# Jensen-Shannon divergence on one core: two first fp32 loads in place of three, products apart from row group 2 on, and new ranges and orders

## Chip, cores and metric

The kernel runs on one core of a Trainium2 chip. The metric is device time in microseconds (us). A profile's span covers the instructions alone and is about 2 us shorter than the time of its run. A run that is more than 1.5% above the fastest of its kernel counts as slow. Medians are over all runs, ratios and their intervals over fast runs alone, and all profiles are of fast runs. Names: ACT is ScalarE, DVE is VectorE, PE is TensorE (PEld its loading of weights), POOL is GpSimd, SP is SyncE.

## The reference

`p` and `q` are 1024 x 4096, fp32.

```python
m = 0.5 * (p + q)
kl_pm = np.sum(p * np.log(p / (m + 1e-8) + 1e-8), axis=-1)
kl_qm = np.sum(q * np.log(q / (m + 1e-8) + 1e-8), axis=-1)
return (0.5 * (kl_pm + kl_qm)).astype(np.float32)
```

The kernel takes log p, log q and log(p+q) apart, so each element pair costs three logs on ACT.

## The kernel before

Eight row groups g of 128 rows; a group's columns are cut into loads, log ranges (for log p and log q together) and sum ranges (for p+q). The order on each engine is written down by hand, one letter per operation:

- `q` (ACT): logs of a range of p and q. `c` (ACT): log of a sum.
- `F` (PE): the sum p+q, by identity matmuls, into one of two PSUM buffers. `a` (DVE): the same for the first fp32 loads.
- `x` (DVE): subtract the logs, then multiply. In "apart" groups `m` (DVE) multiplies inputs and logs, and `s` (DVE) multiplies the sum by its log and reduces.
- `r` (PE): adds a product's columns up in PSUM. `f` (DVE): reduces that to a row's result.

```python
psp = ctx.enter_context(tc.tile_pool(name="psp", bufs=2, space=bass.MemoryType.PSUM))  # sums
AB_BUFS = 3
...
def op_F(j):
    g, c0, w = parts[j]
    st = psp.tile([P, SW], fp32, tag="s")
    v = pq(g, c0, w)
    for b in range(0, w, MMN):
        m = min(MMN, w - b)
        for t in range(2):
            nc.tensor.matmul(out=st[:, b : b + m], lhsT=ident, rhs=v[:, t, b : b + m],
                             start=t == 0, stop=t == 1)
...
def op_m(i):
    g, c0, w = logs[i]
    u = pq(g, c0, w)
    if i < NL - FUSED_LAST:
        nc.vector.tensor_tensor(out=u, in0=u, in1=ab[i], op=Alu.mult)  # over the inputs
        product["m", i] = u
        return
...
def psum_before(j):            # what F(j) needs: its PSUM buffer's last reader
    if j - 2 < HW:
        return []
    return [("s" if apart(parts[j - 2]) else "c", j - 2)]
```

A product `m` is written over the inputs, so it must wait until every `F` that reads those columns is done. And in an apart group a sum `F(j)` must wait until DVE's `s(j-2)` has read the PSUM buffer; in the other groups ACT's `c(j-2)` is enough.

Of the kernel before, what the change touches and what calls it, by code (L numbers as in the profile page):

```python
# [15 lines left out]


LOADS = [
    [256, 320, 384, 512, 704, 832, 1088],
    [1280, 1408, 1408],  # L20
    [1536, 1280, 1280],
    [2048, 2048],
# [3 lines left out]
    [2048, 2048],  # L26
]
LOGS = [
    [256, 320, 384, 512, 704, 832, 1088],
    [1280, 1408, 1408],  # L30
    [1536, 2560],
    [1536, 2560],
    [2048, 2048],
    [768, 1408, 1920],
    [2432, 1664],
    [1664, 1024, 1280, 128],
]
SUMS = [
    [256, 320, 384, 512, 704, 832, 1088],
    [1280, 1408, 1408],  # L40
    [1536, 1408, 1152],
    [1536, 1280, 1280],
    [1152, 1536, 1408],
    [1536, 1152, 1408],
    [1408, 1536, 1152],
    [1280, 1536, 1280],
]
HW = 3

APART = 4  # L50
FUSED_LAST = 1


# [2 lines left out]


ACT_ORDER = """
q0 c0 q1 c1 q2 c2 q3 c3 q4 c4 q5 c5 q6 c6 q7 c7 q8 c8 q9 c9 q10 c10 q11 c11 c12 q12 c13
q13 c14 c15 q14 c16 c17 q15 c18 c19 q16 q17 c20 c21 q18 c22 q19 c23 c24 q20 q21 c25 c26  # L60
q22 q23 c27 q24
"""
PE_ORDER = """
r0 F3 r1 F4 r2 r3 F5 r4 F6 r5 F7 r6 F8 F9 r7 F10 r8 r9 F11 F12 r10 F13 r11 F14 F15 r12 r13
F16 F17 r14 r15 F18 F19 r16 r17 F20 F21 F22 r18 F23 r19 r20 F24 r21 F25 F26 r22 r23 F27
r24 r25
"""
DVE_ORDER = """
a0 a1 x0 a2 x1 x2 x3 x4 x5 x6 x7 f0 x8 x9 x10 f1 x11 x12 x13 f2 x14 x15 s16 s17 m14 m15
s18 s19 m16 m17 s20 s21 f3 f4 m18 s22 f5 m19 s23 s24 m20 m21 s25 s26 m22 f6 m23 s27 f7 m24  # L70
"""


# [1 line left out]
def kernel(  # L75
# [6 lines left out]
    nc = tc.nc  # L82
# [15 lines left out]
    qv = q.rearrange("(p g) d -> g p d", g=n_rg)  # L98
    ov = out.rearrange("(p g) -> p g", g=n_rg)

    def ranges(widths):

        r = []
        for g in range(n_rg):
            col = 0
            for w in widths[g]:
                r.append((g, col, w))
                col += w
            assert col == n_cols
        return r  # L110

    loads, logs, parts = ranges(LOADS), ranges(LOGS), ranges(SUMS)
    assert loads[:HW] == logs[:HW] == parts[:HW]
    split = loads[HW][1]
    NL, NS = len(logs), len(parts)
# [12 lines left out]
    early = []  # L128
    for i in range(HW):
        t32 = small.tile([P, 2, loads[i][2]], fp32, tag=f"pq32_{i}")  # L130
# [6 lines left out]
    def pq(g, c0, w):  # L137
        if g == 0:
            for i in range(HW):
                if loads[i] == (g, c0, w):  # L140
                    return early[i]
            c0 -= split
            assert c0 >= 0
        return data[g][:, :, c0 : c0 + w]
# [4 lines left out]
    nc.vector.memset(epsc_t, SHIFT * 1e-8)  # L149
    for i in range(HW):  # L150
        g, c0, w = loads[i]
        nc.sync.dma_start(out=early[i][:, 0, :], in_=pv[g, :, c0 : c0 + w])
        eng = nc.scalar if i < 2 else nc.sync
        eng.dma_start(out=early[i][:, 1, :], in_=qv[g, :, c0 : c0 + w])
    warm = small.tile([P, 1], fp32, tag="warm")
    nc.scalar.activation(out=warm, in_=tiny_t, func=Act.Ln, bias=tiny_t, scale=1.0)  # L156
    ident = small.tile([P, P], fp16, tag="ident")
    make_identity(nc, ident)
    for g, c0, w in loads[HW:]:
        v = pq(g, c0, w)  # L160
# [4 lines left out]
        out=half, in0=ident, scalar1=0.5, scalar2=0.0, op0=Alu.mult, op1=Alu.add  # L165
# [6 lines left out]

    apart = lambda r: r[0] >= APART
    terms = [("x", j) for j in range(NS) if not apart(parts[j])]
# [105 lines left out]
    def op_f(g):  # L280
        if g < APART:
            nc.vector.tensor_reduce(  # L282
                out=res[:, g : g + 1], in_=acc[g][:, :AW], axis=AX, op=Alu.add
            )
            return
        before, now = next_run(g)
        if g < n_rg - 1:
            now = res[:, g : g + 1]
        junk = small.tile([P, AW], fp16, tag="junk")
        nc.vector.tensor_tensor_reduce(  # L290
            out=junk, in0=acc[g][:, :AW], in1=ones, scale=1.0, scalar=before,
            op0=Alu.mult, op1=Alu.add, accum_out=now,
        )
# [32 lines left out]
    while any(queues):  # L326
        moved = False
        for todo in queues:
            while todo and all(d in emitted for d in after[todo[0][0]](todo[0][1])):
                kind, i = todo.pop(0)  # L330
# [42 lines left out]
```

## Time and profile before

| | before |
|---|---|
| time, median | 106.2 us |
| ACT busy | 93.0 of 103.0 us |
| DVE busy | 82.1 us |
| PE busy | 66.9 us |
| idle of ACT before logs of sums | about 0 |
| loads land until | 85.2 us |

The profiled run took 105.1 us, 1.1 us under the median. From the page of the kernel before: the span, the busy times, the busy tenths of ACT and the granted clock of PE (in tenths of full speed) in 40 slices, and the shares of the chain that ended last.

```profile
span 103.0 us, 1163 instructions
...
PE 66.9 (65%) x412; PEld 41.1 (40%) x412; DVE 82.1 (80%) x87; ACT 93.0 (90%) x55; POOL 22.0 (21%) x46
...
ACT  3736999999999899999999999999999999999900
...
PEclk9999999999999859999966999999669999999995
...
DMA 56%; ACT 23%; issue 12%; POOL 4%; DVE 3%; ACTq 0%; POOLq 0%; DVEq 0%
```

ACT is busy from its start to its end but for the third and fourth slices; its work is the limit. From its timeline (start, duration, instruction, and in brackets the idle time before it and who ended it), the start, the one later wait for a load, and the last log:

```profile
8.63 0.94 ACT L215 ACTIVATE ab_t<-t,tiny_t 128x768 f16<-128x768 f32 x1 [2.47 <-DMA t<-in_q_dram]
...
35.19 4.56 ACT L215 ACTIVATE ab_t<-t,tiny_t 128x5120 f16<-128x5120 f16 x1 [0.28 <-DMA t<-in_q_dram]
...
97.44 0.59 ACT L215 ACTIVATE ab_t<-t,tiny_t 128x256 f16<-128x256 f16 x1
```

In the apart groups DVE runs two products together, and the sums for ACT's next two logs are ready before ACT asks. From the timeline of all engines:

```profile
61.23 4.49 DVE L245 TENSOR_TENSOR t<-t,ab_t 128x4096 f16<-128x4096 f16 x2
61.80 1.02 PE L203 MATMUL st<-t,ident 128*128 128x512 f16 x4
62.84 2.88 ACT L223 ACTIVATE c_t<-st,epsc_t 128x1408 f16<-128x1408 f32 x2
63.57 1.91 PE L272 MATMUL acc_t<-t,half 128*128 128x256 f16 x16 [0.75 <-DVE t L245]
```

The clock of PE falls to a half three times before the end of the work. Busy time in windows around two of them. A line gives the window, its length, the busy us (and number of instructions) of PE, PEld, DVE, ACT and POOL, then the granted clock (1.00 full, 0.50 half), the DMA share and GB/s:

```profile
31.95:35.36 3.41, 1.20 (x12) 1.08 (x12) 2.49 (x3) 3.13 (x3) 1.06 (x2) 1.00 1.10 216
35.36:38.77 3.41, 3.41 (x12) 1.35 (x10) 3.32 (x3) 3.41 (x1) 1.06 (x2) 0.50 1.06 211
...
69.50:72.90 3.40, 1.01 (x6) 0.48 (x5) 3.25 (x5) 3.40 (x4) 0.00 (x0) 1.00 1.06 212
72.90:76.32 3.42, 3.42 (x13) 1.67 (x12) 3.17 (x6) 3.42 (x2) 0.00 (x0) 0.50 1.07 214
```

A window in which PE worked 1.0 to 1.2 us is followed by one at half clock. ACT's busy time there is full: the slow matmuls delay nobody.

### The profile page before, as it was taken

The numbers are of one execution on the slowest core, as the hardware profiler recorded it, in microseconds if no ns is written. First come the engines' busy times: TensorE is split into PE (matmuls) and PEld (weight loads), VectorE is DVE, ScalarE is ACT, GpSimd is POOL, SyncE is SP. The second block draws the span as 40 slices with busy tenths as digits, with TensorE's granted clock in tenths as the row PEclk, the third lists the DMA queues.
The fourth block names the chain that finished last, engine by engine and source line by source line (L and its number), as shares of the span: only waits on it lengthen the run. The fifth ranks groups of instructions, "written<-read, shape, count | busy, mean of one in ns | idle before, by whom it ended". The sixth has DMA issues, their size and how long they took to land.

```text
span 103.0 us, 1163 instructions
## 1 busy us (share of the span) xinstructions
PE 66.9 (65%) x412; PEld 41.1 (40%) x412; DVE 82.1 (80%) x87; ACT 93.0 (90%) x55; POOL 22.0 (21%) x46
## 2 busy tenths in 40 slices
PE   0033986738772798579199877883799649865440
PEld 0010544433432535157154634741268436552330
DVE  2246976669879691999879999999997699799980
ACT  3736999999999899999999999999999999999900
POOL 7935443323232422222222221200000000000000
PEclk9999999999999859999966999999669999999995
DMA  2999999999999999999999999999999920000000
GB/s 76 271 201 183 211 212 214 210 211 210 212 209 217 211 218 212 212 216 210 218 215 212 216 213 212 215 208 221 208 213 218 202 40 6 0 0 0 0 0 2
DMA packets 6773, 17.34 MB, mean 168 GB/s; under 512 B 880, under 2 KB 2416, under 8 KB 6768
## 3 DMA queue, kind: packets, MB, share of 16 engines
q0 software_dynamic: 5760, 16.29, 81.1%
q1 hardware_dynamic: 720, 0.69, 2.3%
q10 hardware_dynamic: 288, 0.30, 0.8%
q8 instruction: 3, 0.05, 0.2%
q14 instruction: 2, 0.02, 0.0%
HBM read 33.55 MB, written 0.00 MB: 326 GB/s over the span
## 4 chain that ended last, share of the span: by engine, by line
DMA 56%; ACT 23%; issue 12%; POOL 4%; DVE 3%; ACTq 0%; POOLq 0%; DVEq 0%
DMA t<-in_p_dram 56%; ACT ab_t L215 14%; ACT c_t L223 8%; POOL t L161 2%; DVE c_t L258 1%; POOL t L162 1%; DVE t L251 0%; DVE junk L290 0%; POOL ident masks.py:199 0%; POOL ident masks.py:197 0%; ACTq L215 0%; DVE t L245 0%; POOLq masks.py:199 0%; DVEq L251 0%; DVEq L290 0%
## 5 line engine op out<-in xcount | busy, mean ns | idle before, releaser
L215 ACT ACTIVATE ab_t<-t,tiny_t 128x2816 f16<-128x2816 f16 (+17 forms) x25 | 62.0, 2500 | 3.3 <-DMA t<-in_q_dram 3.3
L272 PE MATMUL acc_t<-t,half 128*128 128x256 f16 (+1 forms) x260 | 31.8, 273 | 18.2 <-DVE t L238 10.8
L203 PE MATMUL st<-t,ident 128*128 128x512 f16 (+5 forms) x142 | 36.5, 401 | 6.5 <-DVE run L258 3.4
L272 PEld LDWEIGHTS <-half 128*128 128x128 f16 x270 | 26.4, 100 | 35.0 <-issue 29.4
L223 ACT ACTIVATE c_t<-st,epsc_t 128x1408 f16<-128x1408 f32 (+7 forms) x25 | 32.5, 1338 | 0.1
L234 DVE TENSOR_TENSOR ab_t<-ab_t,c_t 128x2560 f16<-128x2560 f16 (+10 forms) x16 | 19.6, 1222 | 7.7 <-ACT c_t L223 7.7
L203 PEld LDWEIGHTS <-ident 128*128 128x128 f16 x142 | 14.9, 109 | 22.9 <-issue 13.8
L238 DVE TENSOR_TENSOR t<-t,ab_t 128x2560 f16<-128x2560 f16 (+7 forms) x13 | 18.1, 1395 | 1.5 <-PE acc_t L272 0.5
L245 DVE TENSOR_TENSOR t<-t,ab_t 128x4096 f16<-128x4096 f16 (+7 forms) x10 | 18.3, 1849 | 0.9 <-ACT ab_t L215 0.9
L161 POOL DMA_DIRECT2D t<-in_p_dram x20 | 10.8, 541 | 23.5 <-DMA t<-in_p_dram 23.4
L162 POOL DMA_DIRECT2D t<-in_q_dram x20 | 10.7, 536 | 20.3 <-DMA t<-in_q_dram 20.3
L258 DVE CUSTOM_DVE_ANT_0 c_t<-st,c_t,run 128x1536 f16<-128x1536 f32 (+3 forms) x8 | 13.2, 1648 | 0.6
L272 PE MATMUL acc_t<-ab_t,half 128*128 128x256 f16 (+2 forms) x10 | 2.1, 356 | 7.6 <-DVE ab_t L238 7.6
L258 DVE CUSTOM_DVE_ANT_0 c_t<-st,c_t 128x1152 f16<-128x1152 f32 (+3 forms) x4 | 6.2, 1554 | 0.0
L191 DVE TENSOR_TENSOR s<-t 128x256 f32<-128x256 f32 (+2 forms) x3 | 1.5, 492 | 4.9 <-DMA t<-in_q_dram 4.9
L290 DVE CUSTOM_DVE_ANT_0 junk<-acc_t,ones,run 128x256 f16<-128x256 f32 x4 | 1.9, 480 | 1.5 <-PE acc_t L272 1.4
L156 ACT ACT_TABLE_LOAD x1 | 1.3, 1283 | 1.7 <-PEq L357 1.7
L238 DVE TENSOR_TENSOR ab_t<-t,ab_t 128x512 f16<-128x512 f32 (+2 forms) x3 | 2.5, 825 | 0.1
L282 DVE TENSOR_REDUCE res<-acc_t 128x1 f32<-128x256 f32 x4 | 1.7, 419 | 0.0
L223 ACT ACTIVATE c_t<-s,epsc_t 128x256 f16<-128x256 f32 (+2 forms) x3 | 1.6, 547 | 0.0
L258 DVE DVE_READ_ACCUMULATOR2_ANT run<- 128x1 f32 x12 | 1.0, 83 | 0.0
L147 DVE MEMSET tiny_t<- 128x1 f32 x1 | 0.1, 59 | 0.8 <-PEq L357 0.8
(14 smaller groups left out, 2.6 us busy)
## 6 DMA issues: line engine op xcount, KB each, us to landing
t<-in_p_dram POOLq DMA_DIRECT2D x10, 512.0 KB, 19.1
t<-in_q_dram POOLq DMA_DIRECT2D x10, 512.0 KB, 19.4
t<-in_p_dram POOLq DMA_DIRECT2D x3, 320.0 KB, 13.2
t<-in_q_dram POOLq DMA_DIRECT2D x3, 320.0 KB, 13.2
t<-in_p_dram POOLq DMA_DIRECT2D x2, 352.0 KB, 10.9
t<-in_q_dram POOLq DMA_DIRECT2D x2, 352.0 KB, 11.6
t<-in_p_dram POOLq DMA_DIRECT2D x1, 384.0 KB, 12.8
t<-in_q_dram POOLq DMA_DIRECT2D x1, 384.0 KB, 13.4
```

The costliest lines, as they stand in the source:

```text
L161: nc.gpsimd.dma_start(out=v[:, 0, :], in_=pv[g, :, c0 : c0 + w])
L162: nc.gpsimd.dma_start(out=v[:, 1, :], in_=qv[g, :, c0 : c0 + w])
L203: nc.tensor.matmul(out=st[:, b : b + m], lhsT=ident, rhs=v[:, t, b : b + m], start=t == 0, stop=t == 1,)
L215: nc.scalar.activation(out=ab_t, in_=pq(g, c0, w), func=Act.Ln, bias=tiny_t, scale=SHIFT)
L223: nc.scalar.activation(out=c_t[:, :w], in_=s[j], func=Act.Ln, bias=epsc_t, scale=SHIFT * 0.5)
L234: nc.vector.tensor_tensor(out=v, in0=v, in1=c[j].unsqueeze(1).to_broadcast([P, 2, w]), op=Alu.subtract)
L238: nc.vector.tensor_tensor(out=into, in0=u, in1=v, op=Alu.mult)
L245: nc.vector.tensor_tensor(out=u, in0=u, in1=ab[i], op=Alu.mult)
L258: nc.vector.tensor_tensor_reduce(out=c[j], in0=s[j], in1=c[j], scale=-0.5, scalar=before, op0=Alu.mult, op1=Alu.add, accum_out=now,)
L272: nc.tensor.matmul(out=acc[g][:, :m], lhsT=half, rhs=v[:, t, b : b + m], start=k == terms_of[g][0] and n == 0, stop=k == terms_of[g][-1] a ...
L282: nc.vector.tensor_reduce(out=res[:, g : g + 1], in_=acc[g][:, :AW], axis=AX, op=Alu.add)
L290: nc.vector.tensor_tensor_reduce(out=junk, in0=acc[g][:, :AW], in1=ones, scale=1.0, scalar=before, op0=Alu.mult, op1=Alu.add, accum_out=now,)
```

## The change

Its intent, read from the diff: start ACT's long run sooner (the first fp32 columns in two loads, p on one hardware queue and q on the other), let DVE wait less for logs of sums in groups 2 and 3, put more log work ahead of the wait for a load near 35 us, and shorten the tail by a last sum of 640 columns. Cut to its core:

```diff
 LOADS = [
-    [256, 320, 384, 512, 704, 832, 1088],
+    [320, 640, 512, 704, 896, 1024],
 ...
 SUMS = [  # LOGS likewise
 ...
-    [1280, 1536, 1280],
+    [1280, 640, 1408, 128, 640],
 ]
-HW = 3
-APART = 4
+HW = 2
+APART = 2
 PE_ORDER = """
-... r10 F13 r11 F14 F15 r12 r13
-F16 F17 r14 r15 F18 F19 r16 r17 F20 F21 F22 r18 F23 r19 r20 ...
+... r10 F13 r11 F14 r12 F15
+F16 r13 F17 F18 r14 F19 F20 r15 F21 F22 r16 F23 F24 r17 ...
 DVE_ORDER = """
-... s16 s17 m14 m15
-s18 s19 m16 m17 s20 s21 f3 f4 m18 ...
+... m10 s11 m11 s12 f2 m12 s13 s14 f3 m13 s15
+s16 m14 s17 s18 f4 m15 ...
@@ first loads
-        eng = nc.scalar if i < 2 else nc.sync
-        eng.dma_start(out=early[i][:, 1, :], in_=qv[g, :, c0 : c0 + w])
+        nc.scalar.dma_start(out=early[i][:, 1, :], in_=qv[g, :, c0 : c0 + w])
```

More of the change, by code (lines that the diff above doesn't have):

```diff
@@ L28 @@
 LOGS = [
-    [256, 320, 384, 512, 704, 832, 1088],
+    [320, 640, 512, 704, 896, 1024],
     [1280, 1408, 1408],
     [1536, 2560],
-    [1536, 2560],
     [2048, 2048],
-    [768, 1408, 1920],
-    [2432, 1664],
-    [1664, 1024, 1280, 128],
+    [2048, 2048],
+    [1920, 2176],
+    [2304, 1792],
+    [1408, 1152, 768, 640, 128],
 ]
 SUMS = [
-    [256, 320, 384, 512, 704, 832, 1088],
+    [320, 640, 512, 704, 896, 1024],
     [1280, 1408, 1408],
+    [1152, 1408, 1536],
+    [1280, 1536, 1280],
+    [1280, 1536, 1280],
     [1536, 1408, 1152],
-    [1536, 1280, 1280],
-    [1152, 1536, 1408],
-    [1536, 1152, 1408],
-    [1408, 1536, 1152],
-    [1280, 1536, 1280],
-]
-HW = 3
-APART = 4
+    [1280, 1280, 1536],
+    [1280, 640, 1408, 128, 640],
+]
+HW = 2
+APART = 2
 FUSED_LAST = 1
 ACT_ORDER = """
-q0 c0 q1 c1 q2 c2 q3 c3 q4 c4 q5 c5 q6 c6 q7 c7 q8 c8 q9 c9 q10 c10 q11 c11 c12 q12 c13
-q13 c14 c15 q14 c16 c17 q15 c18 c19 q16 q17 c20 c21 q18 c22 q19 c23 c24 q20 q21 c25 c26
-q22 q23 c27 q24
+q0 c0 q1 c1 q2 c2 q3 c3 q4 c4 q5 c5 q6 c6 q7 c7 q8 c8 q9 c9 c10 q10 c11 q11 c12 q12 c13
+c14 q13 c15 c16 q14 c17 c18 q15 c19 c20 q16 c21 c22 q17 c23 q18 c24 c25 q19 q20 c26 c27
+q21 q22 c28 q23
 """
 PE_ORDER = """
-r0 F3 r1 F4 r2 r3 F5 r4 F6 r5 F7 r6 F8 F9 r7 F10 r8 r9 F11 F12 r10 F13 r11 F14 F15 r12 r13
-F16 F17 r14 r15 F18 F19 r16 r17 F20 F21 F22 r18 F23 r19 r20 F24 r21 F25 F26 r22 r23 F27
-r24 r25
+F2 r0 F3 r1 F4 r2 r3 F5 r4 F6 r5 F7 F8 r6 F9 r7 F10 r8 r9 F11 F12 r10 F13 r11 F14 r12 F15
+F16 r13 F17 F18 r14 F19 F20 r15 F21 F22 r16 F23 F24 r17 F25 r18 F26 F27 r19 r20 F28 r21
+r22
 """
 DVE_ORDER = """
-a0 a1 x0 a2 x1 x2 x3 x4 x5 x6 x7 f0 x8 x9 x10 f1 x11 x12 x13 f2 x14 x15 s16 s17 m14 m15
-s18 s19 m16 m17 s20 s21 f3 f4 m18 s22 f5 m19 s23 s24 m20 m21 s25 s26 m22 f6 m23 s27 f7 m24
+a0 a1 x0 x1 x2 x3 x4 x5 x6 f0 x7 x8 m9 s9 s10 f1 m10 s11 m11 s12 f2 m12 s13 s14 f3 m13 s15
+s16 m14 s17 s18 f4 m15 s19 s20 m16 s21 s22 f5 m17 s23 m18 s24 s25 m19 f6 m20 s26 s27 m21
+m22 s28 f7 m23
 """
```

## The prediction

> **What bounds it now.** ScalarE. The page gives ACT 93.0 of a 103.0 us span, DVE 82.1, PE 66.9. In the timeline ACT idles only at the start (2.47 us at 6.2-8.6 for the third q load, 0.25 and 0.26 before it) and once for a load (0.28 at 35.2); otherwise it runs until 98.0. A tail of DVE sum, final sum and fused product ends at 100.7, then the store. PE and DVE have slack.
>
> **What the change does.**
> - Loads: same 960 fp32 columns, balanced over two queues. From the landings (3.5, 4.85, 8.54 us) I estimate q1's pair at about 7.2. ACT then reaches column 960 about 0.6 us earlier, but the load that row group 2 waits for (35.08) is DMA-paced; two sum logs now stand before that wait (2560 columns rather than 1536), worth about 0.85 us. Net gain at 35 us: about 0.9 us.
> - ACT: 53 logs and the same columns in both.
> - DVE: groups 2 and 3 swap a subtraction (1.36 us per 2304 elements) for a sum with reduction (1.42 per 1152 columns): about +0.1 us a tile, under 1 us in all.
> - Tail: last sum tile 640 instead of 1280 columns (1.54 us to about 0.85): about 1 us gained.
> - Order, the step that decides. From group 3 on PE has r11 F14 r12 F15 F16 r13 F17 F18: a product's accumulation stands before the sum that the next product waits for (a product overwrites what the sum reads). The sum in turn waits for a PSUM buffer that the DVE reduction frees. So a loop forms: product (2.2 us for 4096 elements) -> its 16 accumulating matmuls (1.9) -> sum F (1.25 to 1.45) -> next product, about 5.5 us with semaphores, while ACT has 4.95 for the same 2048 columns. Before, F stood ahead (F18 F19 r16 r17) and this was hidden.
>
> I laid the three queues out with durations fitted to the old trace; that reproduces the old ACT starts within 0.2 us. For the new order it gives ACT waits for PE sums before c14 (about 1.2 us), c15 (0.7), c16 to c18 (0.4 each): about 3.2 us. Balance: -0.9 -1.0 +3.2 and small terms = +1.7 us at full PE clock.
>
> **Clock.** The old trace shows half clock for 3.41 us at 35.4, 52.4 and 72.9, each just after PE had idled 2.2 to 2.4 us. The Trainium skill, "TensorE: Matmul & The Clock Gate", Part 1, says an idle window of about 3.4 us halves the clock; this trace agrees on the window's length, but a window with 1.0 to 1.3 us of work already did it. The new loop makes PE idle 2.6 us per turn and puts PE on ACT's path, so such windows now cost 1 to 1.5 us each. Three or four of them: +3 to +5 us.
>
> **Prediction: 110.8 us**, range 107.5 to 114.0. Chances: faster 0.07, same 0.15, slower 0.78.
>
> **Right if:** ACT busy stays near 93 us but with 4 to 8 us of idle before sum logs (L223), released by PE sums, between 50 and 95 us; DVE products wait for PE; more half-clock windows after 40 us; the chain of waits alternates PE and DVE there; the tail after the last log is about 1 us shorter; q1's pair lands near 7.2.
>
> **Wrong if:** ACT shows no waits on PE after 40 us (then about 104.3, 1.8% faster), the clock stays full (then about 108).

## The result and the profile after

Ratios in this document are the mean time of one kernel's fast runs over that of the other's fast runs of the same rounds, so not quite the ratio of the medians quoted beside them.

The changed kernel takes 112.72 us (112.35 to 113.17, 4 runs) against 106.23 us in the same rounds: ratio 1.060, 95% interval 1.054 to 1.066. It is slower by 6%, inside the predicted range of 107.5 to 114.0.

The page of the changed kernel, same lines:

```profile
span 110.3 us, 1173 instructions
...
PE 72.3 (66%) x410; PEld 44.5 (40%) x410; DVE 82.5 (75%) x94; ACT 93.9 (85%) x55; POOL 21.9 (20%) x46
...
ACT  4699999999997999992295699899979999599940
...
PEclk9999999999999975595885999999589995898599
...
DMA 28%; PE 20%; issue 18%; ACT 15%; DVE 14%; POOL 2%; ACTq 0%; DVEq 0%; POOLq 0%
```

ACT and DVE have the same work as before to within a microsecond, but ACT now has holes from the middle on, there are more dips of the clock, and PE and DVE, 3% of the old chain together, make up 34% of the new one. The list of waits (who waited for whom: us in total, times, longest) names the holes:

```profile
PE acc_t L272 <- DVE t L245: 17.3, 11, 2.9
...
ACT c_t L223 <- PE st L203: 8.8, 6, 4.2
```

The start and the tail, by the lines that answer to those of before:

```profile
5.52 1.36 ACT L215 ACTIVATE ab_t<-t,tiny_t 128x1280 f16<-128x1280 f32 x1 [0.47 <-DMA t<-in_q_dram]
...
34.46 4.56 ACT L215 ACTIVATE ab_t<-t,tiny_t 128x5120 f16<-128x5120 f16 x1 [0.71 <-DMA t<-in_q_dram]
...
105.63 0.50 ACT L215 ACTIVATE ab_t<-t,tiny_t 128x256 f16<-128x256 f16 x1
```

The second pair of loads lands at 5.5 us and the hole of 2.47 us at the start is gone, but the wait for a load near 35 us grows to 0.71. DVE's last work ends 1.8 us after the last log (107.92 - 106.13), before it was 2.65 (100.68 - 98.03).

The heart of it is this stretch of group 3 (the timeline of all engines, LDWEIGHTS and POOL left out):

```profile
47.49 2.29 DVE L245 TENSOR_TENSOR t<-t,ab_t 128x4096 f16<-128x4096 f16 x1 [3.87 <-issue]
48.76 1.53 ACT L223 ACTIVATE c_t<-st,epsc_t 128x1536 f16<-128x1536 f32 x1
49.70 1.48 DVE L258 CUSTOM_DVE_ANT_0 c_t<-st,c_t 128x1280 f16<-128x1280 f32 x1
49.83 3.46 PE L272 MATMUL acc_t<-t,half 128*128 128x256 f16 x16 [2.01 <-DVE t L245]
...
53.08 1.41 PE L203 MATMUL st<-t,ident 128*128 128x512 f16 x6
54.53 1.33 ACT L223 ACTIVATE c_t<-st,epsc_t 128x1280 f16<-128x1280 f32 x1 [4.24 <-PE st L203]
54.58 2.29 DVE L245 TENSOR_TENSOR t<-t,ab_t 128x4096 f16<-128x4096 f16 x1 [2.99 <-issue]
```

Read from the top: product m11, then its accumulation r11, then the sum F14 behind it on PE, and at F14's end both the log c14 and the product m12 start. The waits of the products say "issue" because the trace does not name who ended them; that m12 starts as F14 ends, and that it must wait for it, is in the order and the code. This turn, from m11 to m12, takes 7.1 us, the next, to m13 at 62.47, takes 7.9: together 15.0 us for the columns of one group. ACT needs 11.0 us for a group where nothing holds it (in the kernel of e9 below, from 39.70 to 50.74). r11's 16 matmuls took 3.46 us, where 16 such matmuls took 1.91 before (63.57 above).

The windows around that stretch, with the clock as above:

```profile
46.57:49.99 3.42, 1.41 (x8) 0.64 (x7) 2.50 (x2) 3.42 (x2) 1.06 (x2) 1.00 1.07 214
49.99:53.40 3.41, 3.41 (x17) 2.33 (x16) 1.60 (x4) 0.30 (x1) 0.53 (x1) 0.50 1.06 213
53.40:56.81 3.41, 1.09 (x6) 0.49 (x5) 2.23 (x2) 2.28 (x2) 0.62 (x2) 1.00 1.06 213
56.81:60.22 3.41, 3.29 (x16) 2.30 (x16) 3.27 (x4) 2.64 (x1) 0.96 (x2) 0.50 1.06 214
...
87.53:90.95 3.42, 0.53 (x6) 0.33 (x4) 2.90 (x2) 3.42 (x3) 0.00 (x0) 1.00 0.00 0
90.95:94.36 3.41, 3.41 (x18) 2.46 (x17) 3.10 (x3) 2.88 (x2) 0.00 (x0) 0.50 0.02 5
```

While PE waits for a product it works little, the clock is halved for the next 3.4 us, and this is when the accumulation runs behind which the sum that ACT waits for has to stand (r11 from 49.83 on). In the window from 49.99 ACT worked 0.30 us.

### The profile page after: what moved, and what is told of

Read it like the earlier page. It is cut to its first block, busy times and chain, and to the rows that moved or that the text cites. A ratio compares the mean times of both kernels' runs of the same rounds, so it can differ in the third digit from the quotient of the medians.

```text
span 110.3 us, 1173 instructions
## 1 busy us (share of the span) xinstructions
PE 72.3 (66%) x410; PEld 44.5 (40%) x410; DVE 82.5 (75%) x94; ACT 93.9 (85%) x55; POOL 21.9 (20%) x46
## 4 chain that ended last, share of the span: by engine, by line
DMA 28%; PE 20%; issue 18%; ACT 15%; DVE 14%; POOL 2%; ACTq 0%; DVEq 0%; POOLq 0%
DMA t<-in_q_dram 28%; PE acc_t L272 14%; ACT ab_t L215 13%; DVE t L245 12%; PE st L203 6%; ACT c_t L223 2%; POOL t L161 1%; DVE c_t L258 1%; DVE junk L290 1%; POOL t L162 0%; DVE t L251 0%; POOL ident masks.py:199 0%; POOL ident masks.py:197 0%; ACTq L215 0%; DVE run L258 0%
## 5 line engine op out<-in xcount | busy, mean ns | idle before, releaser
L215 ACT ACTIVATE ab_t<-t,tiny_t 128x4096 f16<-128x4096 f16 (+18 forms) x24 | 61.4, 2566 | 1.8 <-DMA t<-in_q_dram 1.7
L272 PE MATMUL acc_t<-t,half 128*128 128x256 f16 (+1 forms) x256 | 39.5, 318 | 20.5 <-DVE t L245 17.3
L203 PE MATMUL st<-t,ident 128*128 128x512 f16 (+3 forms) x144 | 35.1, 377 | 13.7 <-DMA t<-in_p_dram 6.7
L272 PEld LDWEIGHTS <-half 128*128 128x128 f16 x266 | 30.1, 115 | 33.2 <-issue 24.2
L223 ACT ACTIVATE c_t<-st,epsc_t 128x1280 f16<-128x1280 f32 (+9 forms) x27 | 32.9, 1236 | 8.8 <-PE st L203 8.8
L245 DVE TENSOR_TENSOR t<-t,ab_t 128x4096 f16<-128x4096 f16 (+10 forms) x14 | 27.7, 1976 | 14.9 <-issue 8.4
L258 DVE CUSTOM_DVE_ANT_0 c_t<-st,c_t,run 128x1536 f16<-128x1536 f32 (+5 forms) x14 | 20.5, 1463 | 1.1
L234 DVE TENSOR_TENSOR ab_t<-ab_t,c_t 128x2816 f16<-128x2816 f16 (+7 forms) x9 | 9.9, 1105 | 3.8 <-ACT c_t L223 3.8
L238 DVE TENSOR_TENSOR t<-t,ab_t 128x2816 f16<-128x2816 f16 (+5 forms) x7 | 8.6, 1235 | 0.6
L258 DVE CUSTOM_DVE_ANT_0 c_t<-st,c_t 128x1280 f16<-128x1280 f32 (+2 forms) x6 | 9.0, 1506 | 0.0
```

Of the source, the lines that this page charges most:

```text
L215: nc.scalar.activation(out=ab_t, in_=pq(g, c0, w), func=Act.Ln, bias=tiny_t, scale=SHIFT)
L223: nc.scalar.activation(out=c_t[:, :w], in_=s[j], func=Act.Ln, bias=epsc_t, scale=SHIFT * 0.5)
L234: nc.vector.tensor_tensor(out=v, in0=v, in1=c[j].unsqueeze(1).to_broadcast([P, 2, w]), op=Alu.subtract)
L238: nc.vector.tensor_tensor(out=into, in0=u, in1=v, op=Alu.mult)
L258: nc.vector.tensor_tensor_reduce(out=c[j], in0=s[j], in1=c[j], scale=-0.5, scalar=before, op0=Alu.mult, op1=Alu.add, accum_out=now,)
L272: nc.tensor.matmul(out=acc[g][:, :m], lhsT=half, rhs=v[:, t, b : b + m], start=k == terms_of[g][0] and n == 0, stop=k == terms_of[g][-1] a ...
```

## The experiments

**Theory.** The new orders tie four operations into a ring: product m waits for the sum F whose inputs it overwrites; F stands behind an accumulation r on PE, and also needs a PSUM buffer that DVE's s frees, and s stands behind m on DVE; r waits for m. The ring is a little slower than ACT, and it starves PE just enough for the clock to halve, which makes it much slower. **Rivals:** the extra reductions of groups 2 and 3 overload DVE; the larger first loads cost it; the accumulation ahead of the sum in PE's order is enough by itself; the clock alone, or not at all.

All 11 experiments gave the right result.

| run | what | time, us (median) | ratio to before (95%) | ACT waits for PE sums, us |
|---|---|---|---|---|
| change | as given | 112.72 | 1.060 (1.054-1.066) | 8.8 |
| e1_both_orders | change, PE and DVE orders new | 104.44 | 0.979 (0.970-0.988) | 0 |
| e2_product_to_log | change, product over its logs | 104.81 | 0.983 (0.973-0.993) | 1.0 |
| e3_loads_only | before, new loads and group 0 | 104.99 | 0.993 (0.986-0.999) | 1.6 |
| e4_extra_matmuls | change, idle matmuls (flawed) | 110.52 | 1.041 (1.031-1.051) | 7.8 |
| e5_zero_matmuls | change, 12 zero matmuls a turn | 105.85 | 0.997 (0.990-1.004) | 3.0 |
| e6_sums_first_pe | change, F ahead of r on PE only | 114.27 | 1.078 (1.070-1.086) | 11.4 |
| e7_ring_in_before | before, ring put into its orders | 110.49 | 1.044 (1.038-1.049) | 3.8 |
| e8_apart_4 | change, APART 4, no ring | 103.16 | 0.973 (0.967-0.978) | 0.9 |
| e9_orders_head | as e1, better head | 102.87 | 0.975 (0.970-0.979) | 0.5 |
| e10_apart_4_again | e8 again | 103.35 | 0.979 (0.974-0.983) | 0.8 |
| e11_zero_4 | as e5, 4 zero matmuls | 105.85 | 1.001 (0.995-1.007) | 2.6 |

Against a limit of 2%, e8 and e9 are faster than the kernel before, e4, e6 and e7 slower, and e3, e5 and e11 the same. e1, e2 and e10 lie below 1 with their whole interval, but whether by 2% is open.

### Both orders altered

```diff
 PE_ORDER
-... F11 F12 r10 F13 r11 F14 r12 F15 F16 r13 F17 F18 r14 F19 F20 r15 ...
+... F11 r7 F12 r8 r9 F13 r10 F14 r11 F15 F16 r12 F17 F18 F19 F20 r13 F21 r14 ...
 DVE_ORDER
-... m10 s11 m11 s12 f2 m12 s13 s14 f3 m13 s15 s16 m14 ...
+... s11 m10 s12 f1 m11 s13 f2 s14 m12 s15 s16 m13 s17 s18 m14 ...
```

> The changed kernel with only the order of PE's and DVE's instructions altered (same ranges, same loads, same operations, products apart from group 2 on). Loop theory (order makes product, its accumulation and the next sum wait for one another in a ring): the ring is gone, ACT's waits for PE sums after 36 us fall from 8.8 us to under 1.5 us, the half-clock windows between 39 and 80 us mostly go, time 103.5 to 105.0 us, faster than the kernel before by 1 to 2.5%. Rival 'the extra reductions of groups 2 and 3 overload DVE': they are all still there, so the time stays at 110 to 113. Rival 'the larger first loads cost it': stays at 112 to 113.

Measured: 104.44 us, by the fast runs 2.1% faster than the kernel before. ACT never waits for a PE sum; after 30 us one half-clock window is left before the end, at 36.6 us. Two early logs wait 1.9 us for accumulations, a flaw of the new head. The extra reductions and the larger loads are all still in this kernel, so neither made it slow.

### One link cut, orders untouched

```diff
-            nc.vector.tensor_tensor(out=u, in0=u, in1=ab[i], op=Alu.mult)
-            product["m", i] = u
+            nc.vector.tensor_tensor(out=ab[i], in0=u, in1=ab[i], op=Alu.mult)
+            product["m", i] = ab[i]
 ...
-            return [("m", i)]                           # who frees a log tile
+            return [("r", terms.index(("m", i)))]
```

> The changed kernel with its orders unchanged, but a product is written over its log tile and no longer over the inputs, so it need not wait for PE's sums that read the inputs. Loop theory: one link of the ring (sum before product) is cut, so ACT's waits for PE sums fall below 2.5 us though r still stands before F in PE's order; time 104 to 107 us. Rival 'an accumulation ahead of a sum in PE's order is enough by itself': time stays above 110. Rival 'DVE overload': stays above 110.

Measured: 104.81 us. Products no longer wait for sums; DVE's products now wait only for ACT's logs, and ACT's waits for PE sums are 1.0 us. From its timeline, the logs c13 and c14, now without a hole between them, and the same product m12 as above, which waits 0.71 us for its logs and not for a sum:

```profile
49.16 2.75 ACT L223 ACTIVATE c_t<-st,epsc_t 128x1536 f16<-128x1536 f32 x2
49.29 2.29 DVE L245 TENSOR_TENSOR ab_t<-t,ab_t 128x4096 f16<-128x4096 f16 x1 [0.71 <-ACT ab_t L215]
```

An accumulation ahead of a sum in PE's order is harmless when the product does not wait for that sum. The wait of m for F is a link that the slowdown needs.

### The loads alone

```diff
-    [256, 320, 384, 512, 704, 832, 1088],     # group 0 of LOADS, LOGS and SUMS
+    [320, 640, 512, 704, 896, 1024],
-HW = 3
+HW = 2
-        eng = nc.scalar if i < 2 else nc.sync
-        eng.dma_start(out=early[i][:, 1, :], in_=qv[g, :, c0 : c0 + w])
+        nc.scalar.dma_start(out=early[i][:, 1, :], in_=qv[g, :, c0 : c0 + w])
 # and the orders of before, renumbered for one range less in group 0
```

> The kernel before with only the new loads, ranges and orders of row group 0. If the loads are harmless or help: first logs reach column 960 earlier, but ACT waits for a load near 35 us, so the time is 0 to 1 us below the kernel before: 105.2 to 106.3. Rival 'the larger first loads cost time': above 107.

Measured: 104.99 us, ratio 0.993: a gain of 0.7%, a little more than expected. ACT waits 1.11 us for the load near 35 us there, so most of the earlier start is lost to that wait. The gain is small: its interval ends at 0.999, and the two profiles (this one and that of the kernel before) both span 103.0 us. The loads are not the cause.

### Work for PE in its idle time: first attempt

```diff
+EXTRA = {j: 12 for j in (12, 13, 14, 16, 18, 20, 22, 24, 25, 27)}
-            acc_t = psa.tile([P, MMN], fp32, tag="acc")
-            acc[g] = acc_t
+            acc[g] = acc2[:, g % 2, :]       # both accumulators in one tile, to free a bank
 ...
+        for _ in range(EXTRA.get(j, 0)):     # at the end of op_F
+            nc.tensor.matmul(out=junk_ps[:, :AW], lhsT=half, rhs=ones, start=True, stop=True)
```

> The changed kernel with 12 idle matmuls of 128x256 (result never read) after the sums that PE used to idle behind, so PE has work in the idle 2.6 us; order of all else as in the changed kernel. If the ring costs about 1 to 2 us at full clock and half-clock windows the rest: granted clock stays at 1.0 from 40 to 100 us, ACT's waits for PE sums fall from 8.8 to about 3.5 us, time 106.5 to 109. Rival 'the ring alone costs it all and the clock is a bystander': time stays within 1 us of 112.7 even at full clock. Rival 'clock alone': time falls to 105 or less.

Measured: 110.52 us, ACT waits 7.8 us, outside what was expected. The trace points to my edit: with both accumulators in one tile, the accumulation of group 2 waited for DVE's reduction of group 1, 3.76 us, ahead of the sum that ACT needed, and that of group 3 later waited 2.51 us in the same way:

```profile
38.02 2.62 PE L276 MATMUL acc<-t,half 128*128 128x256 f16 x12 [3.76 <-DVE res L286]
...
52.90 1.91 PE L276 MATMUL acc<-t,half 128*128 128x256 f16 x16 [2.51 <-DVE res L294]
```

So the time of this run does not tell the clock's share. Its trace does help: the clock was whole from 41.57 to 106.40, and past the two flawed waits ACT's last three holes were 0.51, 0.59 and 0.49 us, the same as in the next run.

### Work for PE in its idle time: repaired

```diff
+        more = EXTRA if 10 <= k <= 20 else 0        # EXTRA = 12
+        for n in range(more):
+            nc.tensor.matmul(out=acc[g][:, :AW], lhsT=zeros, rhs=ones,
+                             start=k == terms_of[g][0] and n == 0, stop=False)
         for n, (t, b) in enumerate(todo):
 ...      # and the real ones start a new sum only where no zeros went before
```

The zeros go into the accumulation itself (r10 to r20), so they wait for nothing that it does not wait for.

> Repair of the run with extra matmuls, whose shared accumulator tile added two waits of PE for DVE. The changed kernel with 12 matmuls of zeros (128x256) added to each accumulation of groups 2 to 6, ahead of the real ones, so that PE has about 1.3 us of work in the idle 2.6 us and no new wait arises; result unchanged. If the ring costs 1 to 2 us at full clock and half-clock windows make up the rest: hardly any half-clock window between 40 and 100 us, ACT's waits for PE sums 3 to 4.5 us (from 8.8), time 107 to 109. Rival 'the clock is a bystander': time within 1 us of 112.7 at full clock. Rival 'clock alone': 105 or less.

Measured: 105.85 us, below what was expected. Two turns of the ring now take 12.4 us (products start at 45.99 and, two later, at 58.34), still more than ACT's 11.0. After 42.4 us the clock is whole to the end of the work (window, clock as above), and ACT's waits for PE sums are 3.0 us in four holes:

```profile
42.40:99.00 56.60, 49.95 (x386) 36.73 (x385) 48.42 (x56) 53.57 (x29) 4.75 (x9) 1.00 0.74 150
```

```profile
ACT c_t L226 <- PE st L206: 3.0, 4, 1.4
```

The time lies just above the 105 of the rival 'clock alone', but the holes of 3.0 us show that the ring still cost time at full clock. So the clock is no bystander: with its order kept, the changed kernel is level with the kernel before (0.997) once PE is kept at work.

### Sums ahead of accumulations on PE alone

```diff
 PE_ORDER
-... F13 r11 F14 r12 F15 F16 r13 F17 F18 r14 ...
+... F13 F14 r11 F15 r12 F16 F17 r13 F18 F19 r14 ...
```

> The changed kernel with one edit in PE's order: from group 3 on each sum stands ahead of the accumulation that preceded it; DVE's order unchanged. My prediction named PE's order as the step that decides; if that alone were the cause, this is enough and the time falls to about 105. If the ring is made by both orders (a sum still waits for a PSUM buffer that DVE frees only after the product, and DVE's final sum f now waits for a later accumulation), it does not help: waits of ACT for PE sums stay at 9 us or more, time 113 to 117.

Measured: 114.27 us, slower than the change itself. From its timeline: product m12, two reductions, a sum that waits for a PSUM buffer until the first of them, the accumulation r12 that stands behind this sum, and DVE's final sum f3, which waits for r12 and holds up product m13:

```profile
51.92 2.29 DVE L245 TENSOR_TENSOR t<-t,ab_t 128x4096 f16<-128x4096 f16 x1 [1.00 <-issue]
...
54.13 1.81 DVE L258 CUSTOM_DVE_ANT_0 c_t<-st,c_t,run 128x1536 f16<-128x1536 f32 x1
56.01 2.31 PE L203 MATMUL st<-t,ident 128*128 128x512 f16 x6 [2.44 <-DVE run L258]
58.11 2.40 PE L272 MATMUL acc_t<-t,half 128*128 128x256 f16 x16
60.55 0.49 DVE L290 CUSTOM_DVE_ANT_0 junk<-acc_t,ones,run 128x256 f16<-128x256 f32 x1 [2.90 <-PE acc_t L272]
61.47 2.29 DVE L245 TENSOR_TENSOR t<-t,ab_t 128x4096 f16<-128x4096 f16 x1 [0.42 <-issue]
```

The ring runs through DVE's order too. The plain repair on PE, which my prediction would have suggested, makes it worse.

### The ring put into the kernel before

```diff
 PE_ORDER
-F16 F17 r14 r15 F18 F19 r16 r17 F20 F21 F22 r18 F23 r19 r20 F24 r21 ...
+F16 F17 r14 F18 r15 F19 r16 F20 r17 F21 r18 F22 r19 F23 F24 r20 r21 ...
 DVE_ORDER
-s16 s17 m14 m15 s18 s19 m16 m17 s20 s21 f3 f4 m18 s22 ...
+s16 m14 s17 m15 s18 f3 m16 s19 m17 s20 f4 m18 s21 s22 ...
```

> The kernel before with nothing changed but the orders of PE and DVE in groups 4 to 7, to alternate as in the changed kernel (product, its accumulation, one sum, next product). Loads, ranges, APART 4 and all operations as before. Loop theory: ACT now waits for PE sums there, 4 to 7 us in all, with half-clock windows after 60 us; time 109.5 to 113. Any rival that blames loads, ranges or the extra reductions: stays at 105.5 to 106.5.

Measured: 110.49 us, ratio 1.044, with no load, range or operation changed. ACT's waits for PE sums are 3.8 us in five holes, one of which (0.51 us at 15.69) lies outside the altered groups; the other 3.3 us are under the expected 4 to 7. In the altered groups, half-clock windows stand at 60.6 and 81.1 us; DVE fell behind as well, and its work ends 3.8 us after the last log (105.77 - 102.02) in place of 2.65. From the list of waits:

```profile
ACT c_t L224 <- PE st L204: 3.8, 5, 1.0
```

The order alone is enough to make the kernel before slow, and by e1 it is what made the changed one slow.

### Products apart from group 4 on, and a better head

The kernel of e8, against the change (LOGS and SUMS of groups 2 and 3 are again those of the kernel before):

```diff
-APART = 2
+APART = 4
 PE_ORDER
-... F13 r11 F14 r12 F15 F16 r13 F17 F18 r14 F19 F20 r15 ...
+... F12 F13 r9 r10 F14 r11 F15 F16 r12 F17 F18 r13 r14 F19 F20 r15 r16 ...
 DVE_ORDER
-... m13 s15 s16 m14 s17 s18 f4 m15 ...
+... x14 s15 s16 m13 s17 f2 s18 m14 s19 f3 s20 f4 m15 ...
 # and small moves in ACT_ORDER
```

The kernel of e9, against e1:

```diff
 PE_ORDER
-F2 F3 r0 F4 r1 r2 F5 r3 F6 r4 ... F13 r10 F14 r11 F15 F16 r12 F17 F18 ...
+F2 r0 F3 r1 F4 F5 r2 F6 r3 ... r10 F13 F14 r11 F15 F16 r12 r13 F17 F18 ...
 DVE_ORDER
-... s11 m10 s12 f1 m11 s13 f2 s14 m12 s15 s16 m13 ...
+... m10 f1 s11 s12 m11 f2 s13 s14 m12 m13 s15 s16 ...
```

> The run with both orders altered had all of the change's parts. Here products apart from group 4 on as in the kernel before (groups 2 and 3 have the ranges of before), with the change's loads, group 0 and groups 4 to 7, and orders again chosen so that no ring forms. If products apart in groups 2 and 3 give nothing by themselves: 104.0 to 105.2, the same as with both orders altered within 0.6 us. If they are worth something: 105.5 or more. If they cost DVE time that matters: below 103.8.

> The changed kernel with other orders of PE and DVE again, in which the accumulation of the first products stays ahead of the second sum (in e1 two early logs waited 1.9 us for it). If that head costs the whole time: 102.6 to 103.8, below e1's 104.4. If the load that ACT waits for near 35 us absorbs it: 103.8 to 104.8, and that wait appears (0.4 to 1 us).

> Repeat of e8 with more rounds beside e9 on one chip. If products apart in groups 2 and 3 are worth nothing either way, within 0.7% of e9; if they cost, e10 is over 0.7% faster than e9. Ratio to the kernel before 0.97 to 0.98.

Measured: e8 103.16 us; then, on one chip in the same rounds, e9 102.87 and e10 103.35. By its own expectation e8 said that products apart in groups 2 and 3 cost time; but e8 was compared with e1, whose head lost 1.9 us. With the head mended, e10 is 0.5% slower than e9, within the 0.7% set beforehand. The two differ in their orders too, so products apart in groups 2 and 3 are worth half a percent at most, and not even the sign is shown. e9, 2.5% faster than the kernel before, is the fastest in the rounds that it shares with e10; e8, the same kernel as e10, had the ratio 0.973 on another chip. From its page and its timeline, the reduction s12 now stands ahead of the product m11 and frees the buffer for F14 in time, and c13 and c14 follow each other without a hole:

```profile
PE 65.3 (65%) x410; PEld 40.0 (40%) x410; DVE 82.2 (81%) x94; ACT 93.3 (92%) x55; POOL 22.0 (22%) x46
```

```profile
44.64 1.49 DVE L258 CUSTOM_DVE_ANT_0 c_t<-st,c_t 128x1280 f16<-128x1280 f32 x1 [1.35 <-ACT c_t L223]
46.06 2.29 DVE L245 TENSOR_TENSOR t<-t,ab_t 128x4096 f16<-128x4096 f16 x1
46.20 1.24 PE L203 MATMUL st<-t,ident 128*128 128x512 f16 x6 [0.99 <-DVE run L258]
48.10 2.75 ACT L223 ACTIVATE c_t<-st,epsc_t 128x1536 f16<-128x1536 f32 x2
```

### Fewer zeros

```diff
-EXTRA = 12
+EXTRA = 4
```

> As e5 with 4 matmuls of zeros rather than 12 per accumulation: about 0.4 us of PE work per turn in place of 1.3 us. If half-clock windows follow stretches of 3.4 us with little PE work: some windows stay, the time lies between e5 (105.9) and the changed kernel (112.7): 107 to 111. If a few matmuls in the gap are enough: 105.5 to 106.5. If they do nothing: 112 or more.

Measured: 105.85 us, the same as with 12, so the expected middle did not come. One half-clock window is left inside the work (40.5 us). With about 0.4 us of added work a turn, the least PE work in one of the clock's 3.41 us windows between 44 and 95 us is 1.45 us, and the clock stayed whole; in the changed kernel 1.41 us was followed by half clock:

```profile
50.73:54.14 3.41, 1.45 (x10) 0.87 (x9) 2.30 (x2) 2.38 (x3) 0.53 (x1) 1.00 1.07 214
```

The 13 traces (the kernels before and after and the 11 experiments), cut into such windows from the first change of the clock (at 11 to 16 us) up to the last whole window, agree with this: all 31 full-clock windows with at most 1.42 us of PE work were followed by half clock, none of the 246 with 1.60 us or more was, and of the 13 between them 3 were (1.54 us before 33.29 in e7 was followed by half clock, 1.46 us before 63.9 in e1 was not).

## Why the prediction was right, and where its terms were off

The direction, the range and the mechanism held: the two ends of the ring were named, the removal of either the order (e1) or one link (e2) takes the loss away, and putting it into the kernel before (e7) makes that slow. That the time came out in the range owes something to luck: the balance at full clock was about 2 us too high (+1.7 against -0.3, from e5's ratio of 0.997) and the clock's term about 2 to 4 us too low, and the two misses offset. Point by point:

- **ACT busy near 93 us with 4 to 8 us of idle before sum logs.** Right in kind: 93.9 us, and 8.8 us of waits.
- **The ring at full clock.** Predicted 3.2 us of ACT waits, first 1.2 before c14; e5 measured 3.0, first 1.43. This term was right. The comparison beside it, 5.5 us a turn against ACT's 4.95, was not: it took a turn with one log of a sum, and turns alternate between one and two. Per group it is 12.4 against 11.0.
- **The clock.** Predicted +3 to +5 us. From the ratios 1.060 (change) and 0.997 (e5), it is 6.3% of 106 us, about 6.7 us. This is the term mis-sized: I counted three or four windows at 1 to 1.5 us each. Six stretches were at half clock after 39 us, and the first held for 6.83 us (39.75 to 46.57): seven windows in all, or about 1 us each (6.7 over 7, an estimate). The size of one was about right, their number was not.
- **"Then about 108" at full clock.** Too high: e5 took 105.85. The gains outside the ring were larger than the 1.9 us that I had summed. e9, which has all of the change without the ring, is 2.5% or about 2.7 us below the kernel before. Of that the tail is 0.80 us (2.65 to 1.85; in the changed kernel 1.79), near the predicted 1. I can't split the rest: the load that ACT waits for near 35 us came late enough for ACT's log to start anywhere between 33.80 (e9) and 35.19 us (before), and with the same first loads at 35.11 (e3) and 33.80 (e9), so single profiles don't settle it.
- **q1's pair near 7.2 us.** Wrong: 5.49. ACT gained it at the start and gave part of it back at 34.46, where it waited 0.71 us.
- **"Order, the step that decides", told as PE's order.** Half right. e6 shows that PE's order alone does not repair it; DVE's order, reductions behind products, is as much a part.

In sum, in shares of the time before: the ring-free change -2.5%, the ring at full clock +2.2 to +2.6% (e5 and e11 against e9), the half clock about +6%. These come from runs of different rounds and are good to about a percent. That windows of little PE work bring the half clock is supported by e5 and e11, which changed only that work, and by the count of windows under e11.

## What to carry to other kernels

When a change moves operations between engines, draw the cycle of waits through all queues (program order, buffers, overwritten inputs) and compare one turn with the limiting engine's time for the same data; a ring a few per cent too slow is enough. An engine with slack is only harmless while others are a step ahead of it: PE ran at half clock in the kernel before too and cost nothing, and cost 6% as soon as ACT waited for it. Cutting one link (here writing the product elsewhere) or reordering both queues repaired it; reordering PE's queue alone made it worse (DVE's alone was not tried).

## What the Trainium skill lacked or had wrong

- "TensorE: Matmul & The Clock Gate", section "HAM oscillation — how this bites in real kernels", gives, as the abstract rule, "no PE-idle gaps >~3.4µs". Here gaps of 2.0 to 2.9 us, in a 3.41 us window with 0.5 to 1.4 us of PE work, were already followed by half clock (windows at 46.57, 53.40 and 87.53 above). The length of the window, 3.41 us, agrees.
- The same page, Part 1, has the clock return after one busy window, but not how busy it must be. In the changed kernel it stayed at a half for a second window after 39.75 us; PE had worked 2.19 us of the first and 3.41 us of the second. In all traces, the clock stayed at a half after the 6 half-clock windows with at most 2.58 us of PE work and returned after the 34 with 2.70 us or more.
- The same page does not say how little work keeps the clock. Here 4 matmuls of 128x256 with zero weights in each idle stretch, about 0.4 us, did (e11), as well as 12 (e5); by the count of windows under e11 the limit lay between 1.42 and 1.60 us of PE work in 3.41 us.
- "Trainium Kernel Development and Optimization", section "Best Practices", says that "consistent bubbles can mean SBUF/PSUM ran out". The bubbles here did run through the two PSUM buffers for sums, but e1 and e2 removed them without another buffer; no page names an order of instructions that holds a buffer too long as a cause.
